# A two-layer transformer kernel whose instructions are put in order on another model of the chip

## The chip, the cores and the metric

One core of a Trainium2 chip runs the whole program. The metric is device time in microseconds (us) of one execution; the kernel before was timed in three runs, and one more execution was profiled.

## The reference

Two layers of a hybrid backbone over 256 latent tokens and 256 context tokens of width 1024, in float32. Each layer norms and modulates the tokens, projects them, runs four branches (retention, window attention, neighbourhood attention, gated delta rule), merges them with gates, and ends with a mixture of 32 experts, of which every token takes two. The second layer computes outputs for the latent tokens only.

```python
def trunk_layer(xl, xc, c, c_ctx, p, w_router, router_bias, cos, sin, ctx_out):
    ...
    hl = modulate(xl, p['norm1'], sh1l, sc1l)
    zl = split_projection(hl @ p['w_in'])
    ...
    ret_c, ret_l = retention_branch(...)
    win_c, win_l = window_branch(...)
    na_c, na_l = neighborhood_branch(...)
    gdn_c, gdn_l = gdn_branch(...)
    xl = xl + g1l * merge_branches(hl, (ret_l, win_l, na_l, gdn_l), p['w_merge'], p['w_branch'], p['w_out'])
    hl2 = modulate(xl, p['norm2'], sh2l, sc2l)
    ...
    y = moe(tokens, w_router, router_bias, p['w_e_gate'], p['w_e_up'], p['w_e_down'])
    xl = xl + g2l * y[b * lc:].reshape(b, l, d)

def moe(h, w_router, router_bias, w_gate, w_up, w_down):
    ...
    def run(args):
        xe, e = args
        return (jax.nn.silu(xe @ w_gate[e]) * (xe @ w_up[e])) @ w_down[e]
```

## The kernel before

`body` (called by `kernel`) traces the program in the order in which the Python code runs; all loops but one are unrolled. Per layer there are three kinds of work.

The dense stage (`dense`): weights come from HBM in pieces of 512 KB (`rawload`, L242), are split into a rounded high part (ScalarE, `split`, L249) and a rest (VectorE or GpSimd, a subtract through the helper `tt`, L177), and three matmuls per product are made of them (`mm3`, L281 to L283), eight products to a PSUM tile (`chunk`, 24 matmuls). Beside these projections and gates run the branches: for the gated delta rule, per pair of heads, a triangular inversion of 31 steps with two VectorE operations each (`gdn_inv`), a block level (`gdn_lev`) and a scan of four steps (`gdn_scan`, matmuls at L960, L964, L971, L983, L985); retention (`ret_head`); and the two attentions (`pair`, scores at L1300, softmax, transposes at L1330). Generators hand out gate and projection chunks between the steps of the branches (`feed`), so that TensorE has other work while a chain of small operations goes on. `merge` multiplies by the branch weights.

The routing stage (`route`, `route_half`): the output projection, the router's logits, and a chain of small VectorE operations that picks experts and places (L177, L183, L1621), then one-hot matrices and the gather matmuls.

The expert stage (`moe`, `mlp`): 16 pairs of experts, each with gate, up and down matmuls against weights that are streamed from HBM through a ring of slots of 1 MB (`expert`, L1849). Its matmuls go through the method `pe` (L165).

What sets the order: five engines work through a queue each, and SP's queue issues the transfers. When the `TileContext` is closed, a scheduler plays the traced program through on a model of the chip. Whenever an engine can take an instruction in that play, it gets, of those whose operands and buffers are ready in the play, the one that was traced first. The order that comes out is each engine's fixed order on the chip, and semaphore waits are added for the operands; the chip keeps the order whatever the real times are. PSUM tiles (pools `pd`, `pk`, `ps` with 2, 2 and 4 buffers) and small SBUF tiles are given out in the same play; most SBUF tensors lie in two arenas whose places are fixed while tracing. Two things tie the order by hand: `keep_in_program_order` (in `pe`) puts a matmul behind everything traced before it on its engine, and `issue_after` puts a block's instructions behind a given one (the transfers in `gdn_xx`, the last scaling of the tokens in `route`, the work after each chunk).

```python
    def pe(self, out, lhs, rhs, start, stop):
        self.tc.keep_in_program_order(self.nc.tensor.matmul(out, lhs, rhs, start=start, stop=stop))
```

## Time and profile before

| | before |
|---|---|
| median of 3 runs | 2506.34 us (2503.37 to 2515.53) |
| profiled execution, its own time | 2507.85 us |
| its span, first to last instruction | 2506.1 us |
| instructions | 38031 |
| TensorE matmul busy | 2319.7 us, 93% of the span |
| TensorE weight load busy | 1590.9 us, 63% |
| VectorE busy | 1330.1 us, 53% |
| ScalarE busy | 815.9 us, 33% |
| GpSimd busy | 519.1 us, 21% |
| moved by DMA | 642.55 MB, mean 256 GB/s |

The first column names a quantity, the second gives it for the profiled execution (the median apart). A busy time is the union of an engine's instructions. Matmuls overlap in the records, so a busy TensorE is not one at its peak. The mean granted TensorE clock over the span was 0.969 of full speed. In the rows further down PE is TensorE, PEld its weight loads, DVE VectorE, ACT ScalarE, POOL GpSimd and SP the engine that issues transfers; L177 is line 177 of the kernel; `<-` in brackets names what ended a wait.

### The profile page before, as it was taken

Reading aid. Unit: us, or ns where it says so; the run is one execution under the profiler, and the core shown is the slowest. Engines: PE = TensorE matmul, PEld = TensorE weight load, DVE = VectorE, ACT = ScalarE, POOL = GpSimd, SP = SyncE. Lnnn points to the kernel's source line nnn. Section 1 sums busy time; section 2 is a strip of 40 time slices with the busy share of each in tenths; the row PEclk is TensorE's granted clock in tenths of the full one; section 3 lists DMA queues with packets and bytes.
Section 4 is the critical chain, followed back from the end, with each engine's and each line's share of the span. In section 5 each row is a group of like instructions: output and inputs, shape, how many; then the busy total and the mean of one; then the engine's idle time right before and its main releaser. Section 6 shows DMA issues by size and latency. Waiting matters only on the chain. (4 is left out here: it accounts for less than half of the span.)

```text
span 2506.1 us, 38031 instructions
## 1 busy us (share of the span) xinstructions
PE 2319.7 (93%) x14396; PEld 1590.9 (63%) x14396; DVE 1330.1 (53%) x3288; ACT 815.9 (33%) x1814; POOL 519.1 (21%) x491
## 2 busy tenths in 40 slices
PE   6989899999989988999999989998899879998897
PEld 4777788766677884444444478988788854433333
DVE  5674754376566666333333468795777652222222
ACT  3443333245455342011011155444477331111010
POOL 3222223231220540111111211011311410000001
PEclk8999999999999988999999989999899989999999
DMA  7335324658637746999999834635336879999997
GB/s 284 112 106 164 102 93 147 229 195 283 212 134 240 230 136 273 403 420 419 419 419 419 327 105 130 200 110 145 93 118 221 265 268 419 419 420 420 420 419 317
DMA packets 269195, 642.55 MB, mean 256 GB/s; under 512 B 64336, under 2 KB 194768, under 8 KB 213072
## 3 DMA queue, kind: packets, MB, share of 16 engines
q1 hardware_dynamic: 269008, 640.07, 69.0%
q8 instruction: 115, 1.88, 0.3%
q14 instruction: 72, 0.59, 0.1%
HBM read 609.85 MB, written 30.16 MB: 255 GB/s over the span
## 5 line engine op out<-in xcount | busy, mean ns | idle before, releaser
L177 POOL TENSOR_TENSOR arenaF<-arenaF 128x512 f32<-128x512 f32 (+3 forms) x224 | 251.2, 1136 | 1214.0 <-DVE arenaF L177 926.9
L281 PE MATMUL pd<-arenaR,arenaR 128*128 128x256 f32 (+1 forms) x1152 | 360.4, 314 | 9.2 <-ACT arenaR L423 3.2
L282 PE MATMUL pd<-arenaR,arenaR 128*128 128x256 f32 (+1 forms) x1152 | 355.8, 309 | 12.3 <-DVE arenaR L177 11.2
L177 DVE TENSOR_TENSOR arenaR<-arenaF,arenaR 128x512 fp32r<-128x512 f32 (+2 forms) x370 | 284.3, 784 | 132.1 <-ACT arenaR L249 107.8
L283 PE MATMUL pd<-arenaR,arenaR 128*128 128x256 f32 (+1 forms) x1152 | 352.7, 306 | 0.0
L249 ACT ACTIVATE arenaR<-arenaF 128x512 fp32r<-128x512 f32 (+1 forms) x348 | 247.0, 721 | 195.0 <-PE pbr L282 55.1
L165 PE MATMUL pw_e_up<-arenaF,arenaF 128*64 128x512 f32 x952 | 225.6, 594 | 20.5 <-DMA arenaF<-in_w_e_up_dram 20.5
L281 PEld LDWEIGHTS pd<-arenaR,arenaR 128*128 128x128 f32 x1152 | 226.1, 197 | 27.6 <-issue 6.3
L282 PEld LDWEIGHTS pd<-arenaR,arenaR 128*128 128x128 f32 x1152 | 226.6, 197 | 23.7 <-DVE arenaR L177 14.9
L283 PEld LDWEIGHTS pd<-arenaR,arenaR 128*128 128x128 f32 x1152 | 226.7, 197 | 10.3 <-issue 4.3
L165 PE MATMUL pw_e_gate<-arenaF,arenaF 128*64 128x512 f32 x944 | 222.8, 598 | 0.0
L177 DVE TENSOR_TENSOR arenaR<-py,arenaR 128x512 fp32r<-128x512 f32 x64 | 44.2, 691 | 310.2 <-ACT arenaR L1924 309.2
L281 PE MATMUL pgate<-arenaR,arenaR 128*128 128x512 f32 (+1 forms) x512 | 177.6, 347 | 2.4 <-ACT arenaF L688 1.4
L165 PE MATMUL py<-arenaF,arenaF 128*64 128x512 f32 x608 | 176.0, 593 | 2.9 <-DMA arenaF<-in_w_e_down_dram 1.9
L283 PE MATMUL pgate<-arenaR,arenaR 128*128 128x512 f32 (+1 forms) x512 | 175.6, 344 | 2.6 <-DVE arenaR L177 2.6
L282 PE MATMUL pgate<-arenaR,arenaR 128*128 128x512 f32 (+1 forms) x512 | 175.3, 343 | 0.0
L165 PEld LDWEIGHTS pw_e_up<-arenaF,arenaF 128*64 128x64 f32 x952 | 71.3, 137 | 161.3 <-issue 124.2
L177 POOL TENSOR_TENSOR arenaR<-arenaF,arenaR 128x1024 fp32r<-128x1024 f32 (+1 forms) x48 | 110.9, 2312 | 188.1 <-ACT arenaR L249 166.4
L177 DVE TENSOR_TENSOR arenaF<-arenaF 128x128 f32<-128x128 f32 (+30 forms) x365 | 131.3, 367 | 7.5 <-ACT arenaF L864 1.8
L1909 ACT ACTIVATE arenaF<-pat 128x512 f32<-128x512 f32 x32 | 19.1, 597 | 356.1 <-PE pat L1907 356.1
L165 PEld LDWEIGHTS pw_e_gate<-arenaF,arenaF 128*64 128x64 f32 x944 | 64.7, 137 | 110.4 <-issue 103.0
L186 DVE SCALAR_TENSOR_TENSOR arenaF<-pw_e_up,ws,arenaF 128x512 f32<-128x512 f32 x32 | 24.0, 751 | 207.1 <-PE pw_e_up L165 207.1
(405 smaller groups left out, 4380.0 us busy)
## 6 DMA issues: line engine op xcount, KB each, us to landing
arenaF<-in_w_e_up_dram SPq DMA_DIRECT2D x119, 1024.0 KB, 18.2
arenaF<-in_w_e_down_dram SPq DMA_DIRECT2D x119, 1024.0 KB, 16.3
arenaF<-in_w_e_gate_dram SPq DMA_DIRECT2D x118, 1024.0 KB, 13.0
arenaF<-in_w_mod_dram SPq DMA_DIRECT2D x48, 1024.0 KB, 6.5
arenaF<-in_w_in_dram SPq DMA_DIRECT2D x92, 512.0 KB, 4.3
arenaF<-in_w_merge_dram SPq DMA_DIRECT2D x64, 512.0 KB, 4.0
arenaF<-in_w_branch_dram SPq DMA_DIRECT2D x32, 512.0 KB, 5.0
arenaF<-in_w_out_dram SPq DMA_DIRECT2D x24, 512.0 KB, 4.6
```

Source lines behind the costliest of these rows:

```text
L165: self.tc.keep_in_program_order(self.nc.tensor.matmul(out, lhs, rhs, start=start, stop=stop))
L177: (eng or self.nc.vector).tensor_tensor(out=out, in0=a, in1=b, op=op)
L186: self.nc.vector.scalar_tensor_tensor(out, a, s, b, op0=op0, op1=op1, accum_out=accum)
L249: self.nc.scalar.activation(h, src, AF.Copy)
L281: mm(ps, L[0], R[0], start=first, stop=False)
L282: mm(ps, L[0], R[1], start=False, stop=False)
L283: return mm(ps, L[1], R[0], start=False, stop=last)
L1909: nc.scalar.activation(aT[:, :, :np_], pt[:, :, :np_], AF.Copy)
```

## The change

One keyword argument, in `kernel`: the scheduler plays the program on a full timeline model (sequencers, queues, the matmul pipeline, transfers that share the DMA engines) where it used its simple model. The traced program, its priorities and the ties by hand are the same.

```diff
--- before.py
+++ after.py
@@ -2110,7 +2110,7 @@
     out = nc.dram_tensor("out_0_dram", (256, D), F32, kind="ExternalOutput").ap()
-    with _tile.TileContext(nc) as tc:
+    with _tile.TileContext(nc, schedule_with_timeline_sim=True) as tc:
         body(tc, aps, out)
     r = _run(nc, [arrays], core_ids=[0])
```

## Rows read from the trace of the kernel before

**Rows 1.** Busy time by stage: us (x instructions), clock, DMA share, GB/s.

```profile
core 0: us, PE busy (x) PEld busy (x) DVE busy (x) ACT busy (x) POOL busy (x), PEclk, DMA share, GB/s
0.00:911.00 911.00, 838.64 (x5480) 666.55 (x5480) 546.13 (x1344) 384.99 (x879) 263.20 (x232) 0.97 0.55 181
911.00:980.00 69.00, 53.14 (x324) 44.62 (x326) 56.65 (x191) 21.37 (x46) 14.36 (x15) 0.78 0.41 149
980.00:1427.00 447.00, 445.11 (x2220) 205.56 (x2218) 152.22 (x266) 44.85 (x76) 74.53 (x60) 1.00 1.01 416
1427.00:2020.00 593.00, 546.68 (x4330) 491.71 (x4327) 433.71 (x1155) 307.76 (x717) 127.72 (x155) 0.96 0.50 154
2020.00:2050.00 30.00, 16.56 (x102) 12.78 (x102) 23.31 (x95) 8.53 (x17) 0.70 (x1) 0.72 0.57 211
2050.00:2506.00 456.00, 419.57 (x1949) 169.70 (x1945) 118.10 (x239) 48.45 (x80) 38.57 (x30) 1.00 0.97 403
```

**Rows 2.** The chain that ended last, from 2130: start, us, what.

```profile
2142.82 17.14 DMA arenaF<-in_w_e_gate_dram
...
2460.83 19.88 DMA arenaF<-in_w_e_up_dram
```

**Rows 3.** PE in order of time, 236 to 250: start, us, what [wait].

```profile
237.19 0.39 PE L281 MATMUL pgate<-arenaR,arenaR 128*128 128x512 f32 x1
237.42 0.40 PE L282 MATMUL pgate<-arenaR,arenaR 128*128 128x512 f32 x1
...
238.15 0.49 PE L971 MATMUL psn<-arenaF,arenaF 128*128 128x128 f32 x2
...
241.88 0.49 PE L960 MATMUL pr<-arenaF,arenaF 128*128 128x128 f32 x2 [1.86 <-DVE arenaF L186]
```

**Rows 4.** Groups: line, engine, what, count, busy us, mean ns, idle.

```profile
L177 DVE TENSOR_TENSOR arenaF<-arenaF 128x128 f32<-128x128 f32 (+30 forms) x365 | 131.3, 367 | 7.5 <-ACT arenaF L864 1.8 <-ACT arenaF L1044 0.2
...
L964 PE MATMUL pxr<-arenaF,arenaF 128*128 128x128 f32 x128 | 24.6, 288 | 0.0
...
L971 PE MATMUL psn<-arenaF,arenaF 128*128 128x128 f32 x96 | 20.3, 293 | 1.1 <-DVE arenaF L186 1.0
```

**Rows 5.** DVE in order of time, 256 to 300.

```profile
267.23 0.34 DVE L186 SCALAR_TENSOR_TENSOR arenaF<-pq,eg,arenaF 128x128 f32<-128x128 f32 x1
267.49 2.31 DVE L177 TENSOR_TENSOR arenaF<-arenaF 128x220 f32<-128x220 f32 x1
...
286.53 9.59 DVE L177 TENSOR_TENSOR arenaF<-arenaF 128x208 f32<-128x208 f32 x25
...
296.66 1.22 DVE L177 TENSOR_TENSOR arenaR<-arenaF,arenaR 128x1024 fp32r<-128x1024 f32 x1
```

**Rows 6.** PE in order of time, 292 to 304.6.

```profile
297.93 0.58 PE L282 MATMUL pd<-arenaR,arenaR 128*128 128x256 f32 x1 [4.74 <-DVE arenaR L177]
...
303.65 0.41 PE L281 MATMUL pd<-arenaR,arenaR 128*128 128x256 f32 x1
303.86 0.41 PE L282 MATMUL pd<-arenaR,arenaR 128*128 128x256 f32 x1
...
304.34 0.28 PE L282 MATMUL pd<-arenaR,arenaR 128*128 128x256 f32 x1
304.46 0.28 PE L283 MATMUL pd<-arenaR,arenaR 128*128 128x256 f32 x1
```

**Rows 7.** The same chain in the second routing stage.

```profile
2039.12 0.13 DVE arenaF L177
2039.26 0.98 DVE arenaR L177
```

**Rows 8.** What PE waited for until 911: us, times, longest.

```profile
PE pd L282 <- DVE arenaR L177: 8.4, 4, 4.7
PE ppt L1330 <- DVE arenaF L186: 7.7, 3, 3.7
```

**Rows 9.** POOL in order of time, 264 to 300.

```profile
267.18 2.36 POOL L177 TENSOR_TENSOR arenaR<-arenaF,arenaR 128x1024 fp32r<-128x1024 f32 x1 [0.72 <-PE pq L985]
```

## The prediction

> **What bounds the kernel now.** I read three views in this order. First the busy table by stage [rows 1]: which engine, or the DMA, is full in which stage. The two expert stages (980 to 1427 and 2050 to 2506 us) move 416 and 403 GB/s with the DMA engines at 1.01 and 0.97 of their time, and in the first of them TensorE has work in 445.1 of 447 us as well. The two dense stages (0 to 911, 1427 to 2020) have the DMA half idle, VectorE at 60 and 73%, and TensorE busy in 838.6 of 911 and 546.7 of 593 us. The two routing stages (911 to 980, 2020 to 2050) are chains of small VectorE operations: VectorE is busy in 56.7 of 69 and 23.3 of 30 us. Then the chain of waits at the end [rows 2]: from 2142.8 to 2480.7 us it is nothing but expert weight transfers, the last stretch of it 19.88 us long and the next transfer right behind each. Last the order on single engines inside the dense stages [rows 3 to 6], because the order is what the change makes anew.
>
> So the program is 903 us that the weight transfers hold, 99 us of routing, and 1504 us in which TensorE is the engine to feed. The reader should see that in the dense stages its recorded idle time is only 911 - 838.6 = 72.4 and 593 - 546.7 = 46.3 us, together 118.7 us [rows 1]: that is what a better order could win back there at most, apart from the clock. There is no such ceiling on what a worse order can lose.
>
> **The change part by part.** No instruction is added or removed, none changes its shape. What changes is which of several ready instructions goes next on PE, DVE, ACT, POOL and in SP's queue of transfers. All terms are set against the profiled execution: span 2506.1, time 2507.85, so 1.75 us lie outside the span; the median of the runs, 2506.34, is 1.51 below that execution, and I shift by that at the end.
>
> Expert stages, 903 us: 0. Each load waits for a weight slot that TensorE frees, and the matmuls there are tied to program order (the method `pe`), so SP's loads keep their order under either model. What hides a change in the DVE, ACT and POOL order is the transfer chain [rows 2]; VectorE is busy in only 152 and 118 us of these stages [rows 1]. Bounds: nothing to gain while the DMA stands at 1.01; if the cover went in the first stage, where TensorE is full too, an engine that comes late by one operation per expert pair would show. I take 0, with +16 us at the upper end (16 pairs at one DVE step of 0.98 us, the nearest row [rows 7]).
>
> Chains with TensorE hops, the `gdn_scan` steps. Their matmuls stand among filler matmuls of a gate chunk: before a hop at 238.15 us one sees filler matmuls 0.23 us apart, and the scan's next matmul then waits 1.86 us for DVE with the rest of the chunk standing behind it in the queue [rows 3]. There are 128 records of the matmuls on `XT` and 96 of those on `kn` [rows 4], eight per step, so 16 and 12 hops; the third kind (`pr`) runs, like the second, in three of four steps: 12 more, 40 in all. A model that lets an engine take on work ahead of its turn, or that thinks a matmul shorter or a DVE answer later, puts more filler in front of a hop. The trace shows no such slip; its bounds are 0 and a whole chunk, 24 matmuls at 0.23 = 5.5 us per hop (below 0 it is the first rival). I take five filler matmuls, 1.2 us, nearest to the run of fillers seen between hops now: 40 x 1.2 = 48 us of chain.
>
> The chain without hops, the triangular inversion in `gdn_inv`, is 4 x 62 = 248 DVE operations among the 365 of a group with a mean of 367 ns [rows 4]. Now other operations (0.34 us) stand singly between two of the chain [rows 5]. A second other operation between two chain operations costs 0.34 us; bounds 0 and 248 x 0.34 = 84 us; I take a quarter, 21 us.
>
> Together the chains get 69 us longer. What hides that is the gate and projection work that TensorE does meanwhile; that work is finite and is used up sooner the longer a chain lasts. I count half as TensorE idle time: +35 us (bounds none and all).
>
> The clock. When TensorE had waited 4.74 us at 297.9 us, its matmuls of 256 columns came 0.21 us apart until about 304.1, and 0.12 us after that [rows 6]: the granted clock was at its lower level of the two, 1.2 GHz instead of 2.4. In 304.1 - 297.9 = 6.2 us it did what takes 6.2 x 0.12 / 0.21 = 3.5 us, a loss of 2.6. Now the dense stages run at 0.97 and 0.96 granted [rows 1]. If the 35 us come as seven waits of this size, they cost 7 x 2.6 = +18 us more (bounds 0 and twice that).
>
> What the new order may mend. At 286.5 us DVE runs 25 inversion operations in a row, 9.59 us; the subtract of a weight split that TensorE's chunk waits for comes only at 296.66 [rows 5, 6]. A model with better times puts it in between. The same two engines meet in four waits, 8.4 us in all, in layer 0 [rows 8], and transposes wait 7.7 us for DVE. I take 12 us off: the 8.4 and half of the 7.7 (bounds 0 and the whole 118.7).
>
> Routing: 0. Its DVE chain has other operations in it already (0.13 of chain, 0.98 of a split) [rows 7], and the longest competitors are tied behind it by `issue_after`. Bounds: ten such splits more or fewer, -10 to +10.
>
> POOL beside DVE. One inversion operation that takes 0.37 us took 2.31 when a POOL subtract of 2.36 us had begun 0.3 us before it [rows 5, 9]. Where such meetings fall is redrawn by the new order, to either side; I take 0 and keep two more or two fewer per inversion, 8 x 1.94 = 16 us, as bounds. The Trainium skill ("SBUF — State Buffer", section "Who interferes with whom") says that a DVE instruction with two SBUF inputs and a GpSimd instruction that reads SBUF exclude each other, and that issue order decides who blocks. The trace agrees, with 2.31 against 0.37 us; by that rule every POOL split that the new order starts ahead of a chain operation is a DVE stall of its length, which would be the +16 end and not 0.
>
> Sum: 35 + 18 - 12 = +41 us, to 2548.9 on the profiled execution and 2547 against the median.
>
> Two readings of TensorE's room differ. Its matmul records leave 118.7 us free in the dense stages; weight loads are busy in only 666.6 of 911 and 491.7 of 593 us [rows 1]. The Trainium skill ("Perfetto Trace Analysis", section "Identifying the Most-Contended Engine") says that matmul busy time is a bad measure of TensorE's room and weight-load time a better one. By it the room would be 244 + 101 = 345 us and the first rival could reach three times as deep; the pitch of 0.12 us inside chunks speaks for the first reading there.
>
> **The rivals.** (1) Faster: a model closer to the chip mends the places where an in-order engine stands behind a late operand with ready work behind it. Place: the subtract behind the inversion, the scan matmul ahead of a waiting chunk (1.86), transposes behind softmax [rows 3, 5, 6, 8]. Price: 8.4 + 7.7 + 1.9 = 18 us, doubled for layer 1, which has the same code at half the rows, makes about 30, and 2.6 for each of some four clock drops: -40 us, 2466. For it: the waits are there, row by row. Against: each is short. It decides the time when the slip per hop is small: half of (40 x s + 21), with the clock loss half as much again, equals 40 us at s = 0.8 us, between three and four filler matmuls.
> (2) No difference: the order that matters is tied (expert matmuls, `issue_after`) and the rest of TensorE's work is chunks of 24 that are ready as a whole, so that both models fill the same holes: 2506, within 12. The flag could also turn out to change next to nothing; the time would be the same. For it: TensorE's waits in the dense stages are short and few [rows 8]. Against: 1504 us hang on thousands of choices.
> (3) Much slower: hops slide behind half a chunk (2.75 us x 40 = 110) and the inversion takes the full 84: half of 194 is 97, clock losses 50: +147, 2653.
>
> **How the numbers follow.** Slower by a few per cent, the forecast: 0.38. (3) and beyond: 0.12. (1): 0.30. (2): 0.20. Slower by over 0.5% is 0.38 + 0.12 = 0.50, within 0.5% 0.20, faster 0.30; 0.5%, 12.5 us, is about what a measurement of this kernel tells from no change. The likeliest case's own range is 2519 to 2620. The range for 8 in 10 runs from 2466, rival (1) at its price, to 2669, rival (3) with the expert stages' upper end: about 1 in 10 lies below it (rival 1 with more than its price) and 1 in 10 above.
>
> **What would show it.** Right: the expert stages again about 447 and 456 us at 416 and 403 GB/s; the dense stages longer, with TensorE idle clearly over 118.7 us in them, waits of scan and inversion behind gate chunks, and a lower granted clock there. Wrong to the fast side: the wait at 297.9 us gone and dense idle under 100 us. Wrong in its foundation: the expert loads leave SP in another order, or DMA falls below 400 GB/s between 980 and 1427, or the dense stages stay as long with another order of everything.

## The result, and the profile after

| | before | after |
|---|---|---|
| median of the runs | 2508.1 us (2503.4 to 2515.5, 4 runs) | 2536.4 us (2531.4 to 2543.5, 4 runs) |
| ratio | 1 | 1.0105, 95% interval 1.009 to 1.0119 |
| profiled execution, span | 2506.1 us | 2541.4 us |
| layer 0, up to its first expert matmul | 967.7 us | 957.2 us |
| layer 1, last transpose of its norm to its first expert matmul | 581.3 us | 624.2 us |

The new order is slower by 28 us, about 1.1%. In the profile one layer gains and the other loses. The busy table by stage, with the bounds moved along with the work (columns as in [rows 1]):

```profile
core 0: us, PE busy (x) PEld busy (x) DVE busy (x) ACT busy (x) POOL busy (x), PEclk, DMA share, GB/s
0.00:900.00 900.00, 847.20 (x5476) 670.63 (x5477) 536.94 (x1343) 381.25 (x876) 254.86 (x233) 0.97 0.55 182
900.00:969.00 69.00, 54.09 (x337) 43.64 (x337) 58.86 (x192) 24.64 (x50) 17.97 (x14) 0.83 0.44 154
969.00:1417.00 448.00, 446.41 (x2219) 206.87 (x2217) 151.19 (x266) 44.79 (x75) 78.67 (x60) 1.00 1.01 416
1417.00:2052.00 635.00, 570.91 (x4323) 507.70 (x4320) 443.61 (x1155) 307.66 (x717) 129.16 (x155) 0.92 0.46 144
2052.00:2085.00 33.00, 19.30 (x111) 15.78 (x111) 26.06 (x109) 9.25 (x18) 0.71 (x1) 0.69 0.52 193
2085.00:2541.00 456.00, 418.75 (x1942) 169.36 (x1938) 113.51 (x226) 47.86 (x79) 38.81 (x30) 1.00 0.97 403
```

Against [rows 1]: the expert stages are the same (448 and 456 us at 416 and 403 GB/s). The dense stage of layer 0 is 11 us shorter, and TensorE's idle time in it falls from 72.4 to 52.8 us. The dense stage of layer 1 is 42 us longer: 17.8 us more of TensorE idle (46.3 to 64.1) and 24.2 us more for the same matmuls (546.7 to 570.9), at a granted clock of 0.92 instead of 0.96.

The next view counts the matmuls of projection chunks (tile `pd`) in stretches of layer 1: up to the first use of the first inverse (`pz`, L911), and beside the first scan. First the kernel before:

```profile
1440.00:1605.00 165.00, 77.00 (x450) 64.13 (x451) 15.59 (x24) 10.01 (x20) 0.96 0.48 139
1626.80:1654.90 28.10, 21.21 (x125) 16.43 (x124) 0.00 (x0) 2.30 (x6) 1.00 0.46 127
```

The same two stretches of the kernel after (columns as above, without POOL):

```profile
1430.00:1632.50 202.50, 97.12 (x624) 86.50 (x624) 15.77 (x24) 12.42 (x26) 0.92 0.47 139
1651.40:1693.90 42.50, 18.01 (x117) 16.13 (x117) 0.00 (x0) 2.33 (x6) 0.80 0.21 60
```

TensorE does 624 instead of 456 such matmuls before it gets to `pz` (the last six of the 456 fall between 1605.0 us, where the first stretch shown ends, and `pz` at 1605.8); the gate chunks ahead of it, 384 matmuls, are the same. Together it is 1008 chunk matmuls ahead of `pz` where it was 840. So the chain (`gdn_at`, inversion, levels, scan) is late: the first inversion begins 125 us after the last transposes of the norm instead of 91. And these chunk matmuls are missing later: from `pz` to the end of the second scan TensorE has 528 of them left instead of 643. What TensorE waits for between 1600 and 1700 us in the kernel after (us in all, times, longest):

```profile
PE pz L911 <- DMA arenaF<-yd: 12.9, 4, 11.2
PE pr L960 <- DVE arenaF L186: 3.8, 4, 2.6
PE pgb L830 <- DVE arenaF L186: 3.1, 7, 0.9
```

In the kernel before the wait of `pz` was 0.7 us. The busy table of the same stretch:

```profile
1600.00:1632.00 32.00, 21.78 (x182) 21.57 (x181) 22.28 (x61) 7.13 (x14) 5.25 (x4) 0.87 0.46 120
1632.00:1700.00 68.00, 54.90 (x523) 47.39 (x524) 47.01 (x144) 18.00 (x40) 7.95 (x10) 0.81 0.22 58
```

and of the answering stretch of the kernel before, where chunks stand beside the scan:

```profile
1605.00:1670.00 65.00, 59.21 (x646) 54.99 (x645) 55.16 (x165) 24.91 (x58) 13.60 (x17) 1.00 0.40 118
```

TensorE is busy in 81 instead of 91% of the time, and the granted clock falls from 1.00 to 0.81.

### The profile page after: what moved, and what is told of

Read it like the earlier page. It is cut to its first block, busy times and chain, and to the rows that moved or that the text cites. A ratio compares the mean times of both kernels' runs of the same rounds, so it can differ in the third digit from the quotient of the medians.

```text
span 2541.4 us, 38134 instructions
## 1 busy us (share of the span) xinstructions
PE 2356.7 (93%) x14396; PEld 1614.0 (64%) x14396; DVE 1330.2 (52%) x3288; ACT 815.4 (32%) x1814; POOL 520.2 (20%) x491
## 4 chain that ended last, share of the span: by engine, by line
PE 64%; DMA 17%; DVE 7%; issue 2%; POOL 1%; ACT 1%; SPq 1%; ACTq 0%; POOLq 0%; DVEq 0%
PE pw_e_gate L165 6%; PE pw_e_up L165 6%; PE py L165 5%; PE pd L281 4%; PE pd L282 4%; PE pd L283 4%; DMA arenaF<-in_w_e_up_dram 4%; DMA arenaF<-in_w_e_down_dram 4%; DMA arenaF<-in_w_e_gate_dram 4%; DVE arenaF L177 3%; PE pcomb L165 3%; PE pgate L281 3%; PE pgate L282 2%; PE pgat L165 2%; PE pgate L283 2%; PE psc L1300 2%
## 5 line engine op out<-in xcount | busy, mean ns | idle before, releaser
L281 PE MATMUL pd<-arenaR,arenaR 128*128 128x256 f32 (+1 forms) x1152 | 354.1, 309 | 9.9 <-ACT arenaR L423 3.2
L282 PE MATMUL pd<-arenaR,arenaR 128*128 128x256 f32 (+1 forms) x1152 | 350.8, 305 | 3.6 <-DVE arenaR L177 2.8
L283 PE MATMUL pd<-arenaR,arenaR 128*128 128x256 f32 (+1 forms) x1152 | 349.8, 304 | 0.0
L177 DVE TENSOR_TENSOR arenaR<-arenaF,arenaR 128x512 fp32r<-128x512 f32 (+2 forms) x370 | 291.1, 802 | 83.5 <-ACT arenaR L249 59.3
L281 PEld LDWEIGHTS pd<-arenaR,arenaR 128*128 128x128 f32 x1152 | 222.5, 194 | 25.6 <-issue 4.3
L282 PEld LDWEIGHTS pd<-arenaR,arenaR 128*128 128x128 f32 x1152 | 222.7, 193 | 17.3 <-issue 5.9
L283 PEld LDWEIGHTS pd<-arenaR,arenaR 128*128 128x128 f32 x1152 | 222.4, 193 | 11.6 <-issue 5.3
L177 DVE TENSOR_TENSOR arenaF<-arenaF 128x256 f32<-128x256 f32 (+30 forms) x365 | 133.3, 375 | 7.9 <-ACT arenaF L1044 1.0
```

The source lines that it names most:

```text
L177: (eng or self.nc.vector).tensor_tensor(out=out, in0=a, in1=b, op=op)
L281: mm(ps, L[0], R[0], start=first, stop=False)
L282: mm(ps, L[0], R[1], start=False, stop=False)
L283: return mm(ps, L[1], R[0], start=False, stop=last)
```

## The experiments

All times below are against runs of the kernel before on the same chip (medians 2508 to 2512 us). The loop for overflowing tokens at the end of layer 0's experts divides the program, so that the two halves are put in order separately. To hold a queue to the order of the other model, the program is built twice, and the second build gets edges of issue order (no waits) between neighbours of the first build's queue:

```python
            for i in bb.instructions:
                k = str(i.engine).split(".")[-1]
                if i.name in names and k in ('PE','DVE','Activation','Pool','SP') and type(i).__name__[4:] in MOVED:
                    if k in last:
                        pairs.append((last[k], i.name))
                    last[k] = i.name
...
            for a, b in tie:
                tc.add_manual_dep(byname[b], a, mybir.DependencyInfo(
                    mybir.DependencyClass.NoSync, mybir.DependencyReason.DATA), reason="order")
```

(`MOVED` lists the kinds of instruction that compute or transfer; `tie` is the list of pairs.)

The table is read from the traces: us after the last transposes of layer 1's norm (`norm_h`) until the first inverse is used (`pz`), until the last matmul on `XT` of the second scan begins, and until the first expert matmul. A row is one execution, the ratio is of medians: the execution shown lies 7 us above the median of its kernel for the kernel after, 9 us above for e2 and 7 us below for e12, and e1 and the kernel before, which have the same order in layer 1, differ by 4 us in the last time.

| kernel | first inverse | second scan ends | first expert matmul | ratio to before |
|---|---|---|---|---|
| e10 (old order, short inversion) | 138.9 | 274.2 | 574.2 | 0.9977 |
| e1 (old order in layer 1) | 139.1 | 277.6 | 577.3 | 0.9956 |
| before | 139.9 | 278.1 | 581.3 | 1 |
| e12 (new order, chunks held) | 152.2 | 293.3 | 598.2 | 1.0008 |
| e11 (old order, chunks ahead) | 167.7 | 300.6 | 605.9 | 1.0087 |
| e5 (old head, then new) | 145.3 | 307.5 | 610.4 | 1.0061 |
| e6 (new head, then old) | 175.0 | 312.8 | 618.1 | 1.0168 |
| e8 (`v` elsewhere) | 176.3 | 322.1 | 621.5 | 1.0123 |
| e9 (new order, short inversion) | 174.0 | 321.1 | 621.6 | 1.0119 |
| e7 (stores off SP) | 172.4 | 318.9 | 624.0 | 1.0107 |
| after | 174.6 | 319.2 | 624.2 | 1.0105 |
| e2 (new order in layer 1 alone) | 172.1 | 322.7 | 628.7 | 1.0169 |
| e3 (TensorE's queue alone) | 170.9 | 326.1 | 641.5 | 1.0233 |
| e4 (VectorE's queue alone) | 176.8 | 331.9 | 654.2 | 1.0267 |

From the end of the second scan to the first expert matmul it is 299 to 306 us in every row but the last two (315 and 322). What the layer loses is lost by then. (e1, e5, e7, e8, e9 and e12 have layer 0's new order too, so their ratios hold its gain.)

**e1 and e2: which layer.**

```diff
-    with _tile.TileContext(nc) as tc:
-        body(tc, aps, out)
...
+    donor, _, names = build(True)
+    nc, arrays, _ = build(False, order(donor, names))
```

with all five queues held, in layer 0 (e1) or in layer 1 (e2).

> All five queues stand in the new model's order up to the end of layer 0's experts and in the old model's order from there on (the loop for overflowing tokens divides the program there). Theory A (the loss is all in layer 1's dense stage, layer 0 gains): layer 0's 10 us of gain alone, about 2496 us, ratio 0.996. Rival (the loss is spread, or layer 1's loss comes from what layer 0 leaves behind): 2506 or more.

Measured: 2498.9 us, ratio 0.9956 (0.9939 to 0.9972).

> The complement: old order up to the end of layer 0's experts, new order from there on. Theory A: the full loss of layer 1 without layer 0's gain, 2508 + 38 to 46 = 2546 to 2554 us. Rival (the two halves hang together): close to the time of the changed kernel, 2536, or below.

Measured: 2554.2 us, ratio 1.0169 (1.0151 to 1.0187). Both as theory A has it: layer 0 gains 11 us, layer 1 loses 42, and the sum is the change (26 us by its ratio) within 5 us. e1 is faster than both kernels.

**e3 and e4: one queue at a time.** As e2, with PE alone (e3) or DVE alone (e4) in the list of queues.

> Old model everywhere, except that in layer 1 TensorE's queue alone is held to the new model's order; the other four queues are put in order again by the old model around it. Theory A1 (the loss lies in TensorE's order: gate chunks issued early, none left beside the scan): 30 to 45 us slower than before, 2538 to 2553. Theory A2 (the loss lies in VectorE's order: other work between the steps of gdn_at and the inversion): within 12 us of before. Theory B (SP's order: stores ahead of weight loads): within 12 us of before.

Measured: 2569.5 us, 1.0233 (1.0216 to 1.025).

> As the run on TensorE's order, but VectorE's queue alone is held to the new model's order in layer 1. Theory A2: 30 to 45 us slower than before, with the inversions of layer 1 at 40 and 44 us instead of 34 and 33. Theory A1: within 12 us, TensorE's chunks fill the longer chains. Theory B: within 12 us of before.

Measured: 2579.7 us, 1.0267 (1.0244 to 1.0291). Either queue alone costs more (58 and 67 us) than all five together (42), which no theory had expected. The first inverse is as late in both as in the kernel after (171 and 177 us): each queue drags the others along, and what is re-made around it fits worse. This way of asking doesn't tell A1 from A2.

**e5 and e6: which part of layer 1.** The five queues are held up to a point (the start of the first inversion) and are free behind it (shown against e2).

```diff
-                    if k in last:
-                        pairs.append((last[k], i.name))
-                    last[k] = i.name
+                    if i.name == CUT[k]:
+                        done.add(k)
+                    pairs.append((last.get(k), i.name))
+                    if k not in done:
+                        last[k] = i.name
```

> New model everywhere, but in layer 1 all five queues are held to the old model's order up to the start of the first inversion (what the kernel before had issued by 1557.0 us); behind that point the new model orders alone. Theory A3 (the loss is made ahead of the first inversion: the chain gdn_ab, gdn_at starts it some 35 us late, because 285 more chunk matmuls are let in front, and those are missing beside the scan): most of the loss is gone, 2500 to 2512 us. Theory A4 (the loss is made behind that point, by splits of weights that stand behind the chain's operations on ACT and VectorE during the scan): 2525 to 2540 us.

Measured: 2526.0 us, 1.0061 (1.0043 to 1.008): 26 us above e1, which has the same layer 0.

> The complement in layer 1, on the old order of layer 0: the new model's order up to the start of the first inversion, the old model's own choice behind it. Theory A3: 2538 to 2555 us. Theory A4: 2500 to 2515 us, since the old model finds filler for the scan again.

Measured: 2553.3 us, 1.0168 (1.0139 to 1.0197). The head alone brings the whole loss, as A3 has it; but the part behind it brings 26 us alone too, as A4 has it. The two don't add up: with a late head, the rest has few chunks left that could be put in its way.

**e7: the stores on SP.** All queues of layer 1 are held to the order of the kernel after but for these stores (`aside` is set in the build that runs).

```diff
-                nc.sync.dma_start(aqd[:, :, 2 * c:2 * c + 2], aq)
+                (nc.gpsimd if l and net_opts['aside'] else nc.sync).dma_start(aqd[:, :, 2 * c:2 * c + 2], aq)
```

> The changed kernel, every instruction in its place, except that the four stores of aqd in layer 1 (line 845) go out by the POOL queue, so that SP's weight loads no longer stand 18.1 us behind the one that waits for the second gdn_at. Theory B: the loads come up to 18 us earlier and the time falls by 10 to 18 us, to 2518 to 2526. Theories A3 and A4: within 5 us of 2536.

Measured: 2539.1 us, 1.0107 (1.0078 to 1.0136), the change's own time. But the waits of SP's queue between 1600 and 1700 us show that the edit only moved the wait (line 858 is the store of `sd`, line 855 of the kernel after):

```profile
SPq L245 <- DVE arenaF L180: 48.7, 7, 16.9
SPq L858 <- DVE arenaF L189: 25.1, 1, 25.1
```

The next store now stands 25.1 us in front of the weight loads. So this run doesn't settle theory B; the next one speaks against it.

**e8: chunks without a bar.** In the kernel after, in e2 and in e6 TensorE stops at exactly 1008 chunk matmuls until the first scan is half through: the retention's `v`, which the next chunk writes, lies where the scan's inputs lay.

```diff
-        v = self.F.alloc((128, 4, 512), *ZIN)
+        v = self.F.alloc((128, 4, 512), *(ZPRJ if l else ZIN))
```

> The changed kernel with one size moved: in layer 1 the retention's v (line 1035) gets storage of its own instead of that of the first scan's inputs, so that TensorE's chunks need not stop at 1008 chunk matmuls until the first scan is through (in the program the scan's first matmul then stands behind 1413 chunk matmuls instead of 1008). Theory A3' (the storage is what costs: TensorE has chunks left, but may not issue them): the idle time and low clock beside the first scan go, 2505 to 2518 us. Theory A5 (the chain gdn_at, inversion, scan sets the end of this stretch; the chunks are finite, and more of them ahead only moves the idle time to the second scan): within 8 us of 2536, or slower.

Measured: 2538.7 us, 1.0123 (1.0106 to 1.0141). The busy table and the longest wait of TensorE behind 1700 us:

```profile
1600.00:1700.00 100.00, 93.50 (x938) 90.79 (x937) 64.23 (x159) 42.07 (x86) 15.32 (x18) 0.98 0.57 152
1700.00:1780.00 80.00, 47.94 (x429) 39.59 (x428) 51.54 (x169) 18.09 (x55) 6.07 (x7) 0.72 0.18 42
```

```profile
PE pz L911 <- DMA arenaF<-yd: 19.8, 4, 18.0
```

The pause beside the first scan is gone, and the same time is lost later, beside the second: the 1536 chunk matmuls that the kernel after has done by the end of its second scan are done by about 1700 us, and TensorE then waits 19.8 us in all (18.0 in one piece) for the second inverse; the clock from 1700 to 1780 us is 0.72. The bar is not the cause (A3' falls). The run speaks against late weight loads (B) too: here the chunks come early, and the time is the same. A5 had expected that time.

**e9 and e10: a shorter inversion.** All queues are held to the order of the kernel after (e9) or before (e10), and in layer 1 each step of the inversions works on one element per partition; the rest of the step is left out (`short` is set in the build that runs).

```diff
+            if l and short[0]:
+                u, n, w = u[:, :1, :1], 1, 1
+                self.tt(u, L[:, j + 1:j + 2, j:j + 1], Y[:, j:j + 1, 0:1], OP.mult)
+                self.tt(Y[:, j + 1:j + 2, 0:1], Y[:, j + 1:j + 2, 0:1], u, OP.subtract)
+                continue
```

> The changed kernel, all five queues of layer 1 held to its own order, but in layer 1 each step of both inversions works on one element instead of up to 256 per partition: that part of the computation is left out, 31 us of VectorE time in the chain (62 operations of 24.9 and 19.7 us in all become 62 of about 0.1 us each). Theory A5 (chain-bound): the time falls by 20 to 31 us, to 2505 to 2516. Theory A6 (TensorE's own work and order bound it, the chain has slack): within 8 us of 2536.

Measured: 2539.6 us, 1.0119 (1.0102 to 1.0135): nothing gained.

> The same cut in the kernel before, with the queues of layer 1 held to its own order: the same two steps of the computation are left out in layer 1. If the old order has the chain covered by chunks (TensorE shows 0 to 2 us idle per 20 us beside both scans), the time falls by less than 8 us from 2508; if the chain bounds the old order as well, it falls by 20 us or more, and Theory A5 then needs the length of the chain, not its cover, to tell the two orders apart.

Measured: 2505.3 us, 0.9977 (0.9963 to 0.999): 6 us gained. The two runs don't decide on A5, because the inversions hardly got shorter. From the first step to the last, layer 1's two take 37.7 and 43.4 us in e9 where they take 40.1 and 44.4 in the kernel after, 3.4 us less in all; in e10 they take 32.1 and 34.6 us where they take 33.8 and 38.5 in the kernel before, 5.6 us less, which is about what the time fell by. Why the first one ends no earlier in e9 is seen in VectorE's rows, its first step and then from 1618 us, first the kernel after (start, us, what; L880 is the copy that follows the inversion):

```profile
1583.56 0.20 DVE L177 TENSOR_TENSOR arenaF<-arenaF 128x31 f32<-128x31 f32 x1
...
1618.40 0.68 DVE L177 TENSOR_TENSOR arenaR<-arenaF,arenaR 128x512 fp32r<-128x512 f32 x1
1619.01 4.66 DVE L177 TENSOR_TENSOR arenaF<-arenaF 128x128 f32<-128x128 f32 x16
1623.70 0.59 DVE L880 COPY arenaF<-arenaF 128x512 f32<-128x512 f32 x1
```

and e9:

```profile
1585.46 0.16 DVE L180 TENSOR_TENSOR arenaF<-arenaF 128x1 f32<-128x1 f32 x1
...
1618.91 0.68 DVE L180 TENSOR_TENSOR arenaR<-arenaF,arenaR 128x512 fp32r<-128x512 f32 x1
1619.51 3.62 DVE L180 TENSOR_TENSOR arenaF<-arenaF 128x1 f32<-128x1 f32 x16
1623.16 0.59 DVE L888 COPY arenaF<-arenaF 128x512 f32<-128x512 f32 x1
```

The copy starts at 1623.70 and at 1623.16. The last 16 steps stand in the queue behind a subtract of a weight split (`arenaR`, 0.68 us) that starts at 1618.40 and 1618.91. During this inversion VectorE waited 3.6 us for ScalarE's halves of these splits and 5.8 us for another result of ScalarE in e9, and 2.0 and 1.0 us in the kernel after; that ScalarE in turn waits for space which TensorE's chunks free is read from the code and not shown. In an order held as it is, the work between the steps sets the pace of the inversion, more than the length of the steps. The saving of VectorE's time was also smaller than the expectation said: a step on one element still takes 160 to 183 ns, not 100, so that about 20 us were taken out and not 31.

**e11 and e12: the chunks alone.** e11 adds a single edge to the kernel before:

```diff
+AHEAD = 1008
...
+    nc, arrays, _ = build(False, [(chunks[AHEAD - 1], first)])
```

(`chunks` are the chunk matmuls in the old order, `first` the first matmul of `pz`). e12 adds one rule to the kernel after (`CHAIN` lists the tiles of the chain's matmuls; the pairs are made from the old order):

```diff
+        for name, tile in pe_of(nc, names):
+            if tile in CHAIN:
+                step = name
+            elif tile in ("pd", "pgate") and step:
+                pairs.append((step, name))
```

> The kernel before with one edge added: in layer 1 the first matmul that uses the first inverse (pz, line 911) may go on TensorE only behind 1008 chunk matmuls, as in the changed kernel, instead of 840; everything else is left to the old model. Theory A6 (the cause is TensorE's queue: 168 more chunk matmuls in front of the chain, about 35 us of it, that are missing beside the scans later): 2535 to 2555 us. Theory A7 (the cause is VectorE's and ACT's order, other work between the steps of gdn_at, inversion and scan; the chunks only follow): 2500 to 2520 us.

Measured: 2535.5 us, 1.0087 (1.006 to 1.0115).

> The changed kernel with one rule added on TensorE in layer 1: no chunk matmul goes ahead of a step of the chain (gdn_ab, gdn_at, the levels, the scan) that stood ahead of it in the old order. The first inverse is then used behind 840 chunk matmuls again, the first scan stands among chunks 895 to 1022; the other four queues stay with the new model. Theory A6: layer 1's loss is gone and layer 0's gain stays, 2498 to 2512 us. Theory A7: 2525 to 2540 us.

Measured: 2512.9 us, 1.0008 (0.9996 to 1.0021). The chunks ahead of the chain cost 22 us where they are put into the old order, and holding them back in the new order wins 24 us (1.0105 less 1.0008 of 2510). That is the larger part of the loss, for which A6 had the whole. Neither edit touches the start alone: in e11 the first inversion still begins 91 us behind the norm and its inverse then waits to be used, and e12's rule also holds chunks behind the later steps of the chain. e12 stays 13 us above e1. Its chain has slower steps although no chunk stands in front of them that didn't before. Two rows of TensorE by line, the transposes of the norm and the second scan from 1725 us on (count, shortest, median and longest duration in ns, first and last start):

```profile
L453 PE MATMUL pxt<-arenaF x64: 362/444/607, 1428.7 to 1447.2; 128*128 128x128 f32 x64
...
L965 PE MATMUL pxr<-arenaF,arenaF x19: 272/275/377, 1724.7 to 1740.6; 128*128 128x128 f32 x19
```

They put the scan's end at 1740.6 - 1447.2 = 293.4 us against 278.1 in the old order. Of these 15 us, 12 are lost before the first inverse is used (152.2 for 139.9): the first inversion takes 43.6 us from its first step to its last instead of 33.8. Beside it VectorE does more subtracts of weight splits and waits more for ScalarE's halves of them, first the kernel before, then e12, whose lines stand one further down (count, busy us and mean ns, idle us before them):

```profile
L177 DVE TENSOR_TENSOR arenaR<-arenaF,arenaR 128x512 fp32r<-128x512 f32 x24 | 16.4, 683 | 0.2 <-ACT arenaR L249 0.2
```

```profile
L178 DVE TENSOR_TENSOR arenaR<-arenaF,arenaR 128x512 fp32r<-128x512 f32 x32 | 21.8, 688 | 4.0 <-ACT arenaR L250 3.9
```

So the 13 us come with the order of the other four queues (A7), and the rows point to VectorE's and ScalarE's; no run here takes the queues apart.

## Why the prediction was right, and where not

The forecast was 2547 us with a range of its own from 2519 to 2620; the median is 2536. Where the loss would be seen (dense stages, clock) and where not (experts, routing) was right. That the sum came so near is in part luck. By it TensorE's idle time in the dense stages rises by 35 - 12 = 23 us and the clock adds 18; in the traces the idle time falls by 1.8 us (118.7 to 116.9), and TensorE's busy time there rises by 32.8 us, 8.6 in layer 0 and 24.2 in layer 1. The mechanism isn't the one forecast either: the prediction has the chains stretched between their steps, and in the runs most of the loss is that layer 1's chain starts late. Its terms, one by one:

- Expert stages, 0: right, 448 and 456 us at the same GB/s. So is routing, 0: 69 us again, and 33 instead of 30.
- Scan hops, +48 us of chain: taken one by one the scans have that size, the cause is right in part. The four scans, first to last matmul on `XT`, take 49.1, 30.9, 42.1 and 29.5 us instead of 34.4, 23.1, 27.7 and 22.3: +44. In layer 0's first scan more chunk matmuls do stand between the hops, as the step says: 197 where there were 67, though these are shorter ones (28.0 us of TensorE's time in all, where the 67 took 22.1). In layer 1's first scan there are fewer, 117 for 125. There VectorE works on the second inversion in the midst of the scan; that this is what lengthens it is argued, no run takes it away. VectorE's `arenaF<-arenaF` operations beside the scan, first the kernel before (count, then busy us and mean ns):

```profile
L177 DVE TENSOR_TENSOR arenaF<-arenaF 128x128 f32<-128x128 f32 (+7 forms) x18 | 4.9, 278 | 0.0
```

after:

```profile
L177 DVE TENSOR_TENSOR arenaF<-arenaF 128x240 f32<-128x240 f32 (+16 forms) x36 | 12.4, 346 | 0.7
```

- Inversion, +21 us: right in sign, about twice too large. From the first step to the last, the two of layer 1 take 40.1 and 44.4 us instead of 33.8 and 38.5, those of layer 0 take 30.8 and 41.6 instead of 34.2 and 38.7: +12 in all. What a shorter inversion would bring in the new order stays open, since e9 made them only 3.4 us shorter.
- Chains 69 us longer, half of it visible: this step failed. From the first inversion's first step to the end of the second scan it takes 218 instead of 204 us in layer 0 and 194 instead of 187 in layer 1: +21 us for both and not 69, since the links overlap more (layer 1's second inversion runs beside the first scan for 23 us instead of 6). Nor is it half that shows. In layer 0 the second scan ends 46 us later and the layer still ends 10.5 us sooner: all is hidden. Presumably its twice as many rows give TensorE enough other work; no run took that work away. In layer 1 the second scan ends 41 us later (319.2 for 278.1) and the first expert matmul 43: all is visible.
- Missing in the sum: the late start of layer 1's chain, which makes 34 of these 41 us (125 for 91). The prediction looked at work between the steps of a chain, not at work in front of its first step. The 168 chunk matmuls there are the largest single cause (22 to 24 us, e11 and e12).
- TensorE idle "clearly over 118.7 us" in the dense stages: wrong in the sum. It is 52.8 + 64.1 = 116.9 us, 19.6 less in layer 0 and 17.8 more in layer 1. Of the other sign one half came (the wait at 297.9 us is gone) and one didn't ("dense idle under 100 us").
- Clock, +18 us: right in kind. By the clock records of the traces the lower level was granted for 96 instead of 44 us of layer 1's dense stage, and TensorE was busy in 68 instead of 38 of them. By the pitches of [rows 6] these 30 us more cost about 30 x (1 - 0.12 / 0.21) = 13 us, an estimate. The other 11 of the 24 us that the same matmuls took longer aren't explained by the clock; in layer 0 too they took 8.6 us longer, with the clock at 0.97 again.
- Mended waits, -12 us: right for the waits that were named, and the size of layer 0's gain (e1: -11). The rows of the kernel after that answer to [rows 8], until 900 us:

```profile
PE ppt L1330 <- DVE arenaF L186: 2.6, 1, 2.6
...
PE pd L282 <- DVE arenaR L177: 2.0, 2, 1.2
```

  7.7 became 2.6 us and 8.4 became 2.0, 11.5 us together; the wait of 4.7 us at 297.9 [rows 6] is gone. That this agrees so well with the gain is in part chance: TensorE's idle time in the layer fell by 19.6 us and its busy time rose by 8.6, other waits went (4.4 us of `pyt` on POOL) and new ones came (11.3 us of `pmod` on VectorE).
- POOL beside VectorE, 0 within 16: right. VectorE's operations of line 177 on `arenaF` alone, the inversion's among them, that ran over 0.6 us beyond the median of their form were 6 with 12.7 us too much before [rows 5, 9] and are 8 with 14.4 us after. The page of the Trainium skill that was weighed there ("SBUF — State Buffer", section "Who interferes with whom") would have allowed the end of +16; the new order didn't go there.

Of the rivals, the first (the new model mends waits) is what layer 0 does, at 11 us instead of 40; the others didn't come. The reading of TensorE's room by the Trainium skill ("Perfetto Trace Analysis", section "Identifying the Most-Contended Engine": judge by weight loads, not by matmul busy time) stays open: weight loads in layer 1's dense stage went from 83 to 80% of the time, which is the direction of the loss, but no run here freed more of TensorE's time than its matmul records showed idle.

## What to carry to other kernels

When an order is made anew, count first how much divisible work stands ahead of the first step of each long chain, and how much is left to stand beside it; the chain's end moved the end of this layer nearly one for one, while taking 20 us of VectorE's work out of two of its links made them only 3 and 6 us shorter, because other work stood between their steps. A fuller model is not a better order everywhere: here one layer gained from it and the other lost, and taking each layer's order from the model that suits it (e1, 2499 us) beat both. One rule on one queue (e12) won back 24 of the 26 us without giving up the new model.

## What the runs showed of the hardware

The clock fell without a long pause. Busy table of the kernel after around the first scan of layer 1 (columns as in [rows 1]):

```profile
1620.00:1640.00 20.00, 6.59 (x191) 5.78 (x192) 6.17 (x23) 0.85 (x3) 0.00 (x0) 0.60 0.51 103
1640.00:1660.00 20.00, 14.43 (x111) 10.04 (x108) 13.19 (x46) 4.47 (x8) 5.69 (x8) 0.93 0.05 16
1660.00:1680.00 20.00, 15.84 (x79) 13.52 (x78) 13.09 (x41) 4.53 (x10) 0.45 (x1) 0.62 0.23 53
```

The first drop goes with the wait of 11.2 us for the inverse. Then the clock was back at 0.93, and it fell to 0.62 again behind a stretch in which TensorE was busy in 14.4 of 20 us and never waited longer than 0.9 us. The kernel before was busy in 19.5 of 20 us between 1640 and 1660 and had 1.00. Over the whole dense stage of layer 1 the lower of the two levels (1.2 instead of 2.4 GHz) was granted for 96 us, and for 44 in the kernel before.

A VectorE operation on one element per partition, among long ones, took 183 ns on average in e9 (62 of them 11.3 us in the first inversion of layer 1); the group with the full steps, on 16 to 256 elements, has a mean of 337 ns in the kernel after (74 operations, 12 of them not steps of the inversion). Making the operations 16 to 256 times smaller saved about half of their time.
